# Binary cross-entropy over 8192 x 8192: the first block of predictions loaded by two queues, 64 rows each

## The chip, the cores and the metric

The kernel runs on one core of one Trainium2 chip. The metric is the device time of one execution in microseconds (us). A profile is taken of one further execution, with its own time.

## The reference

```python
def reference(pred, target):
    eps = 1e-7
    pred = np.clip(pred, eps, 1 - eps)
    return -(target * np.log(pred) + (1 - target) * np.log(1 - pred))
```

Both inputs are 8192 x 8192 fp32; `target` holds only zeros and ones. So each element of the result is -log(pred) where the target is 1 and -log(1 - pred) where it is 0. The kernel uses that: it forms |target - 1 + pred|, which is pred or 1 - pred, takes the logarithm and changes the sign.

## The kernel before, in words

The 67,108,864 elements are taken as one flat row and cut into 40 chunks. Chunk `k` is a contiguous stretch of memory, laid out as 128 rows (one for each partition of the on-chip memory) of `widths[k]` elements: two first chunks of 5,120 columns, 35 of 14,336 (`BIG`), two of 5,632 and one of 1,024. Predictions live as fp32 in `ring_p`, which has three slots of 14,336 columns and a small one; the result is made in place there and stored from there. Targets live in `ring_t`, one slot of 14,336 columns and a small one, as bf16: the load converts them, so it reads twice the bytes it writes. The first two chunks lie side by side in one slot of each ring.

The order is written out by hand; nothing is scheduled. For each chunk:

- `load_p` (L69) and `load_t` (L72) bring in predictions and targets. Both are issued by GpSimd (POOL), with one exception: the predictions of chunk 0 are issued by SyncE (SP). All that POOL issues goes through one queue, q0, in the order of issue; SP's transfers use a hardware queue, q1.
- `clip` (L85) on VectorE (DVE).
- `log`: on DVE target - 1 + pred (L91), then on ScalarE (ACT) Abs (L94) and Ln (L95).
- `back` (L99) on DVE multiplies by -1.
- `store` (L76), issued by POOL, for the last chunks by SP. The last chunk goes out by `store_rows` (L81) as three transfers of 108, 12 and 8 rows.

A big chunk is computed in two halves of 7,168 columns. `load_t(k + 1)` stands behind the last L91 of chunk `k`, because there is only one big slot for targets; `load_p(k + 2)` stands behind `store(k)`, since POOL issues in order.

The start, which the change touches, is: a memset of `warm` on DVE; on POOL `load_t(0)`, `load_t(1)`, `load_p(1)`, `load_p(2)`; on SP `load_p(0)`; on ACT a logarithm of `warm` (L108), which loads the table of the function early. Then chunks 0 and 1 are clipped and their logarithms taken, `load_t(2)` is issued, then the sign of chunk 0 is changed and it is stored, and the same for chunk 1.

In what follows p0, p1, p2 are the predictions of chunks 0, 1, 2, and t0, t1, t2 their targets.

Of the kernel before, what the change touches and what calls it, by code (L numbers as in the profile page):

```python
# [1 line left out]

# [4 lines left out]

EPS = 1e-7

BIG = 14 * 1024  # L10
FIRST = 5 * 1024
LAST = 5632
TAIL = 1024
SLOTS = 3


def plan(total):
    n = (total - 2 * FIRST - 2 * LAST - TAIL) // BIG
    assert n > 4 and total == 2 * FIRST + n * BIG + 2 * LAST + TAIL
    spots = [(FIRST, 0, 0), (FIRST, FIRST, FIRST)]  # L20
    spots += [(BIG, k % SLOTS * BIG, 0) for k in range(1, n + 1)]
    end = (n + 1) % SLOTS * BIG
    spots += [(LAST, end, 0), (LAST, end + LAST, LAST)]
    return spots + [(TAIL, SLOTS * BIG, BIG)]


@with_exitstack
def kernel(
    ctx: ExitStack,
    tc: tile.TileContext,  # L30
    pred: bass.AP,
    target: bass.AP,
    out: bass.AP,
):
    nc = tc.nc
    fp32 = mybir.dt.float32
    bf16 = mybir.dt.bfloat16
    Alu = mybir.AluOpType
    Act = mybir.ActivationFunctionType
    P = nc.NUM_PARTITIONS  # L40

    R, C = pred.shape
    spots = plan(R * C // P)
    n = len(spots)
    widths = [s[0] for s in spots]
    cols = [sum(widths[:k]) for k in range(n)]

    def chunk(ap, k):
        flat = ap.rearrange("r c -> (r c)")
        return flat[cols[k] * P : (cols[k] + widths[k]) * P].rearrange("(p w) -> p w", p=P)  # L50

    pool = ctx.enter_context(tc.tile_pool(name="rings", bufs=1))
    ring_p = pool.tile([P, SLOTS * BIG + TAIL], fp32, name="ring_p", tag="ring_p")
    ring_t = pool.tile([P, BIG + TAIL], bf16, name="ring_t", tag="ring_t")
    warm = pool.tile([1, 8], fp32, name="warm", tag="warm")

    def spot(k, part=(0, 1)):
        w, c, _ = spots[k]
        i, m = part
        return ring_p[:, c + i * w // m : c + (i + 1) * w // m]  # L60

    def spot_t(k, part=(0, 1)):
        w, _, c = spots[k]
        i, m = part
        return ring_t[:, c + i * w // m : c + (i + 1) * w // m]

    def load_p(k):
        queue = nc.sync if k == 0 else nc.gpsimd
        queue.dma_start(out=spot(k), in_=chunk(pred, k))  # L69

    def load_t(k):
        nc.gpsimd.dma_start(out=spot_t(k), in_=chunk(target, k))  # L72

    def store(k):
        queue = nc.sync if k >= n - 3 else nc.gpsimd
        queue.dma_start(out=chunk(out, k), in_=spot(k))  # L76

    def store_rows(k):
        src, dst = spot(k), chunk(out, k)
        for first, last in ((0, 108), (108, 120), (120, 128)):  # L80
            nc.sync.dma_start(out=dst[first:last], in_=src[first:last])  # L81

    def clip(k, *part):
        p = spot(k, *part)
        nc.vector.tensor_scalar(  # L85
            out=p, in0=p, scalar1=EPS, scalar2=1 - EPS, op0=Alu.max, op1=Alu.min
        )

    def log(k, *part):
        p = spot(k, *part)  # L90
        nc.vector.scalar_tensor_tensor(  # L91
            out=p, in0=spot_t(k, *part), scalar=1.0, in1=p, op0=Alu.subtract, op1=Alu.add
        )
        nc.scalar.activation(out=p, in_=p, func=Act.Abs)  # L94
        nc.scalar.activation(out=p, in_=p, func=Act.Ln)  # L95

    def back(k, *part):
        p = spot(k, *part)
        nc.vector.tensor_scalar(out=p, in0=p, scalar1=-1.0, scalar2=None, op0=Alu.mult)  # L99

    with tc.manual_schedule():
        nc.vector.memset(warm, 1.0)  # L102
        load_t(0)
        load_p(0)
        load_t(1)
        load_p(1)
        load_p(2)
        nc.scalar.activation(out=warm, in_=warm, func=Act.Ln)  # L108
        for k in (0, 1):
            clip(k)  # L110
            log(k)
        load_t(2)
        back(0)
        store(0)
        back(1)
        store(1)
        load_p(3)
        a, b, c = range(n - 3, n)
        for k in range(2, n - 3):
            for h in (0, 1):  # L120
                clip(k, (h, 2))
                log(k, (h, 2))
            if k < n - 4:
                load_t(k + 1)
            else:
                load_t(a)
                load_t(b)
                load_p(c)
                load_t(c)
                back(k, (0, 2))  # L130
                for j in (a, b):
                    clip(j)
            if k < n - 4:
                back(k, (0, 2))
            back(k, (1, 2))
            store(k)
            if k + 2 < n - 3:
                load_p(k + 2)
            elif k + 2 == n - 3:
                load_p(a)  # L140
                load_p(b)
        log(a, (0, 2))
        log(a, (1, 2))
        clip(c)
        log(b, (0, 2))
        back(a, (0, 2))
        log(b, (1, 2))
        back(a, (1, 2))
        store(a)
        log(c)  # L150
        back(b, (0, 2))
        back(b, (1, 2))
        store(b)
        back(c)
        store_rows(c)


# [1 line left out]
_INS = ['pred', 'target']  # L159
_OUTS = [((8192, 8192), 'float32')]  # L160


# [23 lines left out]
```

## Time and profile before

| | |
|---|---|
| median of 3 runs | 1864.81 us (1864.67 to 1865.51) |
| profiled execution, its own time | 1864.33 us |
| its span, first to last instruction | 1862.6 us |
| DVE busy | 1121.6 us, 60% |
| ACT busy | 902.4 us, 48% |
| POOL busy | 178.5 us, 10% |
| bytes read from HBM, written to it | 536.87 MB, 268.44 MB: 432 GB/s over the span |
| DMA queue q0 (POOL) | 16,704 packets, 662.18 MB, 99.1% of the engines' span |
| DMA queue q1 (SP) | 592 packets, 8.91 MB, 1.1% |

The page names queues by number. A packet of data is one row of a transfer; a few packets of 4 bytes report that a transfer has landed. The column GB/s counts bytes as they are written, so that a load of targets (fp32 read, bf16 written) counts half of what it reads. "DMA" is the mean busy share of the core's 16 DMA engines. "Idle before, releaser" in a line of the timeline is the time for which the engine stood idle before the instruction, and what ended it.

### The profile page before, as it was taken

To read this page: it belongs to the slowest core of one execution; us is meant where nothing else is said; L and a number is where in the kernel's file an instruction comes from. 1 tells how busy PE (TensorE), PEld (TensorE's weight loads), DVE (VectorE), ACT (ScalarE), POOL (GpSimd) and SP (SyncE) were. 2 spreads that over 40 slices of the span, in tenths; PEclk is the share of its full clock that TensorE was granted. 3 is DMA by queue.
4 is the path that set the end of the run, shared out by engine and by line. 5 is a ranking of instruction groups with operands and counts; after the bars stand their busy time and mean duration, and the time that the engine had idled before them with its cause. 6 is when DMAs were issued, how large, how long until landed. Compare 5 with 4: busy or idle time off the path is not lost.

```text
span 1862.6 us, 707 instructions
## 1 busy us (share of the span) xinstructions
DVE 1121.6 (60%) x230; ACT 902.4 (48%) x156; POOL 178.5 (10%) x120
## 2 busy tenths in 40 slices
DVE  4666555555666566555555666566655555666565
ACT  4454444455555544444455555544444445555545
POOL 1111101111110011101111110011101111110020
DMA  9999999999999999999999999999999999999999
GB/s 346 347 371 355 356 352 355 356 355 354 359 375 374 375 372 355 355 355 355 355 355 355 357 374 374 374 372 355 355 356 355 357 357 356 357 373 376 375 352 356
DMA packets 17302, 671.15 MB, mean 360 GB/s; under 512 B 1936, under 2 KB 1936, under 8 KB 2320
## 3 DMA queue, kind: packets, MB, share of 16 engines
q0 software_dynamic: 16704, 662.18, 99.1%
q1 hardware_dynamic: 592, 8.91, 1.1%
q14 instruction: 6, 0.05, 0.0%
HBM read 536.87 MB, written 268.44 MB: 432 GB/s over the span
## 4 chain that ended last, share of the span: by engine, by line
DMA 60%; issue 35%; ACT 3%; DVE 2%; POOL 0%; POOLq 0%; DVEq 0%; PEldq 0%
DMA ring_t<-in_target_dram 57%; DMA ring_p<-in_pred_dram 4%; ACT ring_p L95 1%; ACT ring_p L94 1%; DVE ring_p L91 1%; DVE ring_p L99 0%; DVE ring_p L85 0%; POOL out_dram L76 0%; POOL ring_t L72 0%; POOLq L72 0%; POOL ring_p L69 0%; POOLq L76 0%; DVEq L91 0%; PEldq L181 0%
## 5 line engine op out<-in xcount | busy, mean ns | idle before, releaser
L94 ACT ACTIVATE ring_p<-ring_p 128x7168 f32<-128x7168 f32 (+3 forms) x77 | 452.0, 5870 | 942.1 <-DVE ring_p L91 942.1
L91 DVE SCALAR_TENSOR_TENSOR ring_p<-ring_t,ring_p 128x7168 f32<-128x7168 bf16 (+3 forms) x77 | 558.2, 7251 | 372.5 <-DMA ring_t<-in_target_dram 371.3
L99 DVE TENSOR_SCALAR ring_p<-ring_p 128x7168 f32<-128x7168 f32 (+3 forms) x77 | 285.4, 3706 | 329.4 <-ACT ring_p L95 329.4
L95 ACT ACTIVATE ring_p<-ring_p 128x7168 f32<-128x7168 f32 (+3 forms) x77 | 452.5, 5877 | 2.4
L85 DVE TENSOR_SCALAR ring_p<-ring_p 128x7168 f32<-128x7168 f32 (+3 forms) x75 | 284.6, 3794 | 24.0 <-DMA ring_p<-in_pred_dram 24.0
L76 POOL DMA_DIRECT2D out_dram<-ring_p x37 | 128.0, 3459 | 584.4 <-DVE ring_p L99 584.3
L72 POOL DMA_DIRECT2D ring_t<-in_target_dram x40 | 28.9, 722 | 1057.5 <-DVE ring_p L91 1056.7
L69 POOL DMA_DIRECT2D ring_p<-in_pred_dram x39 | 21.7, 558 | 2.5 <-issue 2.5
L108 ACT ACT_TABLE_LOAD x1 | 1.3, 1283 | 0.7 <-PEq L170 0.7
L102 DVE MEMSET warm<- 1x8 f32 x1 | 0.1, 65 | 0.8 <-PEq L170 0.8
L108 ACT ACTIVATE warm<-warm 1x8 f32<-1x8 f32 x1 | 0.2, 208 | 0.0
L170 POOL MEMSET const-float32-0.0<- 128x1 f32 x1 | 0.1, 99 | 0.2 <-issue 0.2
L170 POOL MEMSET const-bfloat16-1.0<- 128x1 bf16 x1 | 0.1, 102 | 0.0
L170 POOL MEMSET const-float32-1.0<- 128x1 f32 x1 | 0.1, 99 | 0.0
L170 POOL MEMSET const-uint8-127<- 128x1 uint8 x1 | 0.1, 99 | 0.0
## 6 DMA issues: line engine op xcount, KB each, us to landing
ring_p<-in_pred_dram POOLq DMA_DIRECT2D x35, 7168.0 KB, 44.3
out_dram<-ring_p POOLq DMA_DIRECT2D x35, 7168.0 KB, 31.1
ring_t<-in_target_dram POOLq DMA_DIRECT2D x35, 3584.0 KB, 31.3
ring_p<-in_pred_dram POOLq DMA_DIRECT2D x2, 2816.0 KB, 37.2
out_dram<-ring_p SPq DMA_DIRECT2D x2, 2816.0 KB, 14.7
out_dram<-ring_p POOLq DMA_DIRECT2D x2, 2560.0 KB, 28.7
ring_t<-in_target_dram POOLq DMA_DIRECT2D x2, 1408.0 KB, 26.5
ring_p<-in_pred_dram SPq DMA_DIRECT2D x1, 2560.0 KB, 13.1
```

The source lines that it names most:

```text
L69: queue.dma_start(out=spot(k), in_=chunk(pred, k))
L72: nc.gpsimd.dma_start(out=spot_t(k), in_=chunk(target, k))
L76: queue.dma_start(out=chunk(out, k), in_=spot(k))
L85: nc.vector.tensor_scalar(out=p, in0=p, scalar1=EPS, scalar2=1 - EPS, op0=Alu.max, op1=Alu.min)
L91: nc.vector.scalar_tensor_tensor(out=p, in0=spot_t(k, *part), scalar=1.0, in1=p, op0=Alu.subtract, op1=Alu.add)
L94: nc.scalar.activation(out=p, in_=p, func=Act.Abs)
L95: nc.scalar.activation(out=p, in_=p, func=Act.Ln)
L99: nc.vector.tensor_scalar(out=p, in0=p, scalar1=-1.0, scalar2=None, op0=Alu.mult)
L102: nc.vector.memset(warm, 1.0)
L108: nc.scalar.activation(out=warm, in_=warm, func=Act.Ln)
L170: nc = _bacc.Bacc("TRN2", target_bir_lowering=False, num_devices=1)
```

## The change

p0 is loaded by two transfers instead of one. SyncE issues rows (partitions) 0 to 63, ScalarE rows 64 to 127, both at the start; each half is 1,310,720 bytes in rows of 20,480 bytes. On ScalarE the issue stands ahead of the load of the function table and of the logarithm of `warm`. Whoever used the whole of p0, or the slot after it, now waits for two transfers instead of one. Everything else, the order on DVE, POOL and SP included, is as before.

```diff
     def load_p(k):
-        queue = nc.sync if k == 0 else nc.gpsimd
-        queue.dma_start(out=spot(k), in_=chunk(pred, k))
+        if k == 0:
+            for i, queue in enumerate((nc.sync, nc.scalar)):
+                half = slice(i * P // 2, (i + 1) * P // 2)
+                queue.dma_start(out=spot(0)[half], in_=chunk(pred, 0)[half])
+        else:
+            nc.gpsimd.dma_start(out=spot(k), in_=chunk(pred, k))
```

## The prediction

> **What bounds the kernel now.** I read the page first: the strip of 40 slices and the table of queues.
>
> ```profile
> span 1862.6 us, 707 instructions
> DMA  9999999999999999999999999999999999999999
> q0 software_dynamic: 16704, 662.18, 99.1%
> q1 hardware_dynamic: 592, 8.91, 1.1%
> HBM read 536.87 MB, written 268.44 MB: 432 GB/s over the span
> ```
>
> The transfer engines are busy from end to end, while VectorE, the busiest compute engine, is at 60%. To see whether anything could leave them idle I took the medians from issue to landing, and two windows of the middle of the kernel, one period of a big chunk each.
>
> ```profile
> ring_p<-in_pred_dram POOLq DMA_DIRECT2D x35, 7168.0 KB, 44.3
> ring_t<-in_target_dram POOLq DMA_DIRECT2D x35, 3584.0 KB, 31.3
> ...
> 455.18:505.92 50.74, 31.07 (x7) 24.60 (x4) 5.09 (x4) 1.00 1.00 362
> 505.92:556.66 50.74, 30.57 (x7) 24.60 (x4) 4.59 (x4) 1.00 1.00 361
> ```
>
> A period moves 7.34 MB of predictions, 7.34 MB of targets (as read) and 7.34 MB of results: 22.02 MB in 50.74 us, 434 GB/s, or 27.1 GB/s for each of 16 engines; one of the three takes 16.9 us. A load of targets that lands 31.3 us after its issue has therefore waited 14 us behind other transfers, a load of predictions 27 us. So the queue is never empty, and the kernel is one long line of transfers: a step on a compute engine that comes a few us sooner or later changes nothing, and a microsecond that the transfer engines lose at the start is missing at the end. What counts is whether the change costs or gives transfer time. For that I read the first 60 us of the timeline and short windows (the last two columns are the engines' share and GB/s).
>
> ```profile
> 0.74 0.40 SPq L69 DMA_DIRECT2D ring_p<-in_pred_dram  x1
> ...
> 13.88 2.83 DVE L85 TENSOR_SCALAR ring_p<-ring_p 128x5120 f32<-128x5120 f32 x1 [13.02 <-DMA ring_p<-in_pred_dram]
> 16.74 5.49 DVE L91 SCALAR_TENSOR_TENSOR ring_p<-ring_t,ring_p 128x5120 f32<-128x5120 bf16 x1
> ...
> 28.36 2.83 DVE L85 TENSOR_SCALAR ring_p<-ring_p 128x5120 f32<-128x5120 f32 x1 [6.12 <-DMA ring_p<-in_pred_dram]
> ...
> 37.00 2.57 POOL L72 DMA_DIRECT2D ring_t<-in_target_dram  x1 [33.51 <-DVE ring_p L91]
> ```
>
> ```profile
> 2.00:3.00 1.00, 0.00 (x0) 0.23 (x2) 1.00 (x3) 1.00 0.61 184
> 3.00:4.00 1.00, 0.00 (x0) 0.00 (x0) 0.49 (x1) 1.00 1.02 430
> 4.00:5.00 1.00, 0.00 (x0) 0.00 (x0) 0.00 (x0) 1.00 0.91 389
> 5.00:6.00 1.00, 0.00 (x0) 0.00 (x0) 0.00 (x0) 1.00 1.01 307
> 6.00:12.00 6.00, 0.00 (x0) 0.00 (x0) 0.00 (x0) 1.00 1.00 316
> ```
>
> p0 runs alone from about 2 us. At 5 to 6 us GB/s falls: the targets, which count half, have come in from POOL's queue. From 6 to 12 us 316 GB/s at a share of 1.00 is a mixture: with 434 for predictions and 217 for targets, 46% of the engines' time goes to p0, so the two queues take about equal turns. p0 lands at 13.9 us. Then VectorE waits 6.12 us for p1.
>
> **The change part by part.**
>
> *What it gives on paper.* With two queues of three, p0 gets two turns of three instead of one of two. Sharing starts near 5.5 us and ends at 13.9; the same bytes then need three quarters of those 8.4 us, so p0 lands 2.1 us sooner. The clip (2.83 us) starts sooner by as much, but t0 has the place that p0 gave up: the two together have the same bytes as before. By the trace t0 was issued at 1.24 us and landed 14.9 us later, at 16.1, so the first L91 moves from 16.74 to 16.1 at best. ScalarE starts 0.6 us sooner, and all of it ends in the 6.12 us wait for p1, which lands after t0, p0 and t1 whatever their order. Gain on the path: 0.
>
> *ScalarE's issue.* One issue of about 0.40 us (SyncE's row) stands ahead of the table load (1.28 us at 0.73) and the warm logarithm (0.21 us at 2.03). These would end at 2.6 us instead of 2.2; ScalarE's next work waits for L91 until 22.27, so 20 us cover it. Uncovered it would be 0.4 us. The new waits for two transfers where there was one (clip 0, the first Abs, POOL's first store) cost a step of the sequencer, 0.02 us in the chain's rows, all beside running transfers. The time around the span, 1864.33 - 1862.6 = 1.73 us, I leave as it is; no row shows what a second hardware queue adds there.
>
> *The front of the transfers.* From 2 to 3 us the share is 0.61, so 0.39 us is lost, and by the packet records the sixteen first packets take 1.23 us on average instead of 0.76, another 0.5. A second queue could fill some of this: 0 to -0.9 us. It needs the same sixteen engines to start, so I take 0.
>
> *Half-height transfers.* This is the part that decides. How many engines serve a half? q1's 592 packets tell: p0 and the two SyncE stores of 128 rows, and the last chunk's 128 rows, are 512 data packets. Of the 80 left, three transfers of 128 rows with one report from each of 16 engines make 48; the other 32 are the transfers of 108, 12 and 8 rows: 12 + 12 + 8, in each case the largest number up to 16 that divides the rows. 64 rows therefore go to all 16 engines, four rows each. Before, sixteen engines wrote 128 rows at a time, each its own eight; now, whenever their turns coincide, sixteen write into the same 64 rows, and two engines share what one had. If the rows' side takes 27 GB/s for each such group, two engines that are on the same half at once run at half speed. p0 is 2.62 MB, 6.04 us at 434 GB/s. So the cost lies between 0 (the rows' side has room, or the engines always take opposite halves) and +6.04 us (they are always on the same half). The nearest row is the stretch of the last stores, the only ones with fewer rows: 363 GB/s from 1858 to 1860 us at a share of 0.88, or 412 GB/s at full share, 5% under 434. It is near the lower end, but it is a row of reads from the chip's memory, in 4 KB packets, while the engines run out of work, and I don't take it for 20 KB writes. Two queues that start within half a microsecond with the same turn on every engine make coinciding turns the more frequent case, so between half (3.0) and all (6.0) I take three quarters: +4.5 us. Nothing hides it: the line of transfers has no gap to absorb it.
>
> The Trainium skill has a rule that speaks against the change. "SBUF — State Buffer", section "Door 1: The DMA port swizzle", gives 8 of 16 ports for partitions 0 to 63, with 196 GB/s measured at 1 MiB against 328 for 128 partitions, and its section on two DMAs to both halves says that two at once were only 6% faster than one. By that p0 would move at some 208 GB/s, an estimate from that page: 12.6 us instead of 6.04, and the end +6.6 us. No row here shows it.
>
> *What is late next.* p1 would land 4.5 us later, at 32.8; L85 and L91 follow, and t2 is issued at 41.5 instead of 37.00. p2 was issued at 2.95 and took 42.3 us, to 45.2, so t2 had 8.2 us in hand, less the time from issue to first bytes (t0: 1.24 to about 5.5, 4.3 us): 3.9. p2 ends later by the same 4.5, so the margin stays, and no gap is added.
>
> Sum against the profiled execution: 1864.33 + 0 + 0 + 0 + 4.5 = 1868.8 us. Its own time is 0.48 below the median of the runs, so the median could as well come out at 1869.3; I keep 1868.8.
>
> **The rivals.**
>
> *The halves add up* (not slower). If engines on the same half don't hinder each other, every term is 0: 1864.3, or 1864.8 by the median. For it: the equal turns of 6 to 12 us cost no share, and the last stores' row above. Against it: that row is all there is on few rows, and in all full-speed rows each engine has rows of its own. Chance 0.33.
>
> *The front fills faster.* Both sequencers feed the engines, the 0.9 us go: 1863.4. For it the share of 0.61; against it that all 16 engines serve one transfer already. Chance 0.05.
>
> *Both halves on the same eight engines.* If 64 rows went to eight engines, the same for both queues, those would carry 12.08 us of p0 instead of 6.04 and stay 6.04 us behind the others to the end, since every later transfer gives all engines equal shares: 1870.4. It decides as soon as the eight lag by more than the end's 2 us of thin work (share 0.88). Against it is the count of reports. Chance 0.03.
>
> *Something at the front that I don't see makes it faster by over 0.2%.* All that precedes full speed is 2.0 + 0.9 = 2.9 us, under 0.2% (3.7 us). Chance 0.03.
>
> **How the numbers follow.** 0.2%, 3.7 us, is about what a measurement of this kernel can tell from no change. The forecast's case has 0.56: its cost is spread from about 2 to 6.04, and from 62% of p0's packets colliding (3.7 of 6.04) it counts as slower; I give that 0.48 and what lies below 0.08. Slower: 0.48 + 0.03 = 0.51. Same: 0.08 + 0.33 + 0.05 = 0.46. Faster: 0.03. The forecast's own range is 1866.4 to 1870.4. The range for 8 in 10 takes in the rival of no cost, from 1863.9, and the upper bound with the spread of the runs, to 1870.6; both signs of the question lie in it.
>
> **What would show it.** Right: from 2 to 15 us the packets of p0 take longer than 0.76 us and GB/s at full share is well under 389 (2 to 5 us) and 316 (6 to 12 us); p1's clip starts near 32.8 instead of 28.36; from there every row is later by the same amount up to the last store. Wrong: p1's clip at 28.4 and the same period of 50.74 us, with clip 0 at about 11.8. The forecast is also wrong if the front is slow but the lag is gone by the end: then the line of transfers has a gap that I didn't find. A period other than 50.74 would mean that the change reaches beyond the start, for which I see no way.

## The result, and the profile after

| | median, us | runs | against the kernel before, same series |
|---|---|---|---|
| before, with the first series | 1864.81 | 9, 1864.36 to 1865.51 | |
| the change, first series | 1871.27 | 9, 1868.98 to 1878.75 | 1.0041 [1.0033, 1.0049] |
| the change, second series (e5_again) | 1870.17 | 8, 1869.35 to 1871.36 | 1.0027 [1.0017, 1.0037] |
| the change, third series (e8_third) | 1869.83 | 10, 1868.85 to 1870.41 | 1.0025 [1.0016, 1.0035] |

The change makes the kernel slower: by 6.5 us in the first series, by 4.9 in each of the two others (before: 1865.23 and 1864.94). The first series has four runs above 1872 us, the two others none; these four count in its ratio, which is above that of the medians (1.0035). Its profile is that of its slowest run, 1878.75 us with a span of 1877.0.

The page of the changed kernel, strip and queues. (The change moves the lines of the text: the clip is L89 here, target - 1 + pred is L95, `load_t` L76, and p0 is loaded by L71.)

```profile
span 1877.0 us, 713 instructions
DMA  9999999999999999999999999999999999999997
q0 software_dynamic: 16704, 662.18, 98.4%
q1 hardware_dynamic: 528, 7.60, 1.2%
q10 hardware_dynamic: 80, 1.31, 0.3%
HBM read 536.87 MB, written 268.44 MB: 429 GB/s over the span
```

ScalarE's half is q10: 1.31 MB in 80 packets, 64 of data and 16 reports, so 16 engines served 64 rows, as counted in the prediction. The line of transfers is as full as before, and slower. The start of the timeline, and the windows over it (last two columns: the engines' share and GB/s):

```profile
0.73 0.55 ACTq L71 DMA_DIRECT2D ring_p<-in_pred_dram  x1
0.73 0.58 SPq L71 DMA_DIRECT2D ring_p<-in_pred_dram  x1
...
19.05 2.83 DVE L89 TENSOR_SCALAR ring_p<-ring_p 128x5120 f32<-128x5120 f32 x1 [18.19 <-DMA ring_p<-in_pred_dram]
21.91 5.49 DVE L95 SCALAR_TENSOR_TENSOR ring_p<-ring_t,ring_p 128x5120 f32<-128x5120 bf16 x1
...
33.30 2.83 DVE L89 TENSOR_SCALAR ring_p<-ring_p 128x5120 f32<-128x5120 f32 x1 [5.90 <-DMA ring_p<-in_pred_dram]
...
41.95 2.57 POOL L76 DMA_DIRECT2D ring_t<-in_target_dram  x1 [38.47 <-DVE ring_p L95]
```

```profile
2.00:3.00 1.00, 0.00 (x0) 0.81 (x2) 1.00 (x3) 1.00 1.48 328
3.00:4.00 1.00, 0.00 (x0) 0.00 (x0) 0.48 (x1) 1.00 1.44 307
4.00:5.00 1.00, 0.00 (x0) 0.00 (x0) 0.00 (x0) 1.00 0.50 102
5.00:6.00 1.00, 0.00 (x0) 0.00 (x0) 0.00 (x0) 1.00 1.20 246
6.00:12.00 6.00, 0.00 (x0) 0.00 (x0) 0.00 (x0) 1.00 0.93 205
```

Packets count in the window in which they start; over 2 to 6 us the four rows make 0.98 MB, 246 GB/s (328 before), and from 6 to 12 us 205 instead of 316. By the packet records a 20 KB row of p0 takes 1.39 to 1.60 us (medians of sixteen after sixteen) where it took 0.76 to 0.78 after each engine's first one. The mean times of these eight groups of sixteen add up to 11.96 us instead of 6.64: that is what an engine spends on its eight rows. p1's clip, which waits for all that stands ahead of it, comes at 33.30 instead of 28.36: 4.94 us later, and t2 is issued 4.95 later.

So the start costs 4.9 us in a run that is 14.4 us longer than the one before (1864.33). The rest came later. Two targets' loads from the chain that ended last (start in us, length), of the profile before, of this one, and of the third series':

```profile
485.50 31.34 DMA ring_t<-in_target_dram
...
1703.12 31.25 DMA ring_t<-in_target_dram
```

```profile
490.67 31.49 DMA ring_t<-in_target_dram
...
1713.26 32.00 DMA ring_t<-in_target_dram
```

```profile
489.91 31.20 DMA ring_t<-in_target_dram
...
1707.45 31.19 DMA ring_t<-in_target_dram
```

They are 24 chunks apart: a period of 50.73 us before, 50.94 in the first series' profile and 50.73 in the third's. In the first series' profile the load at 490.67 is 5.2 us later than before and the one at 1713.26 is 10.1 us later; the other 4.3 of the 14.4 us come behind it, up to the end.

### The profile page after: what moved, and what is told of

It is laid out like the page before. It is cut to its first block, busy times and chain, and to the rows that moved or that the text cites. A ratio compares the mean times of both kernels' runs of the same rounds, so it can differ in the third digit from the quotient of the medians.

```text
span 1877.0 us, 713 instructions
## 1 busy us (share of the span) xinstructions
DVE 1121.6 (60%) x230; ACT 902.4 (48%) x156; POOL 178.4 (10%) x120
## 3 DMA queue, kind: packets, MB, share of 16 engines
q10 hardware_dynamic: 80, 1.31, 0.3%
## 4 chain that ended last, share of the span: by engine, by line
DMA 60%; issue 35%; ACT 2%; DVE 1%; POOL 0%; POOLq 0%; DVEq 0%; PEldq 0%
DMA ring_t<-in_target_dram 58%; DMA ring_p<-in_pred_dram 2%; ACT ring_p L99 1%; ACT ring_p L98 1%; DVE ring_p L95 1%; DVE ring_p L103 0%; POOL out_dram L80 0%; DVE ring_p L89 0%; POOL ring_t L76 0%; POOLq L76 0%; POOL ring_p L73 0%; POOLq L80 0%; DVEq L95 0%; PEldq L185 0%
## 5 line engine op out<-in xcount | busy, mean ns | idle before, releaser
L95 DVE SCALAR_TENSOR_TENSOR ring_p<-ring_t,ring_p 128x7168 f32<-128x7168 bf16 (+3 forms) x77 | 558.2, 7251 | 378.4 <-DMA ring_t<-in_target_dram 377.1
L89 DVE TENSOR_SCALAR ring_p<-ring_p 128x7168 f32<-128x7168 f32 (+3 forms) x75 | 284.6, 3794 | 29.3 <-DMA ring_p<-in_pred_dram 29.3
L76 POOL DMA_DIRECT2D ring_t<-in_target_dram x40 | 28.9, 722 | 1068.4 <-DVE ring_p L95 1067.6
```

The lines of the kernel that those rows point to most:

```text
L89: nc.vector.tensor_scalar(out=p, in0=p, scalar1=EPS, scalar2=1 - EPS, op0=Alu.max, op1=Alu.min)
L95: nc.vector.scalar_tensor_tensor(out=p, in0=spot_t(k, *part), scalar=1.0, in1=p, op0=Alu.subtract, op1=Alu.add)
```

## The experiments

Ratios are to the kernel before, run beside each.

**e1_columns: two queues, whole height.**

```diff
-                half = slice(i * P // 2, (i + 1) * P // 2)
-                queue.dma_start(out=spot(0)[half], in_=chunk(pred, 0)[half])
+                half = slice(i * FIRST // 2, (i + 1) * FIRST // 2)
+                queue.dma_start(out=spot(0)[:, half], in_=chunk(pred, 0)[:, half])
```

> p0 by two queues as in the change, but cut by columns: SyncE loads columns 0 to 2559 of all 128 rows, ScalarE the other 2560. Same two queues, same bytes. Theory A (sixteen engines writing into 64 rows go at half speed): packets are whole height again, so no cost: p1's clip at 28.4 +- 0.5 us as before (33.30 with the change), median 1864.3 to 1865.5. Rival B (a second hardware queue at the start costs, whatever it carries): p1's clip near 33 us and the median 1869 to 1873 as with the change. Rival C (what is late at the end comes from two queues setting the engines' order, not from the rows): p1's clip near 28.4 but runs spread over several us.

1865.33 us (1864.69 to 1866.52), ratio 1.0001 [0.9992, 1.0010]. Windows and timeline:

```profile
4.00:5.00 1.00, 0.00 (x0) 0.00 (x0) 0.00 (x0) 1.00 1.06 451
5.00:6.00 1.00, 0.00 (x0) 0.00 (x0) 0.00 (x0) 1.00 1.11 338
6.00:12.00 6.00, 0.00 (x0) 0.00 (x0) 0.00 (x0) 1.00 1.02 324
```

```profile
28.54 2.83 DVE L89 TENSOR_SCALAR ring_p<-ring_p 128x5120 f32<-128x5120 f32 x1 [5.96 <-DMA ring_p<-in_pred_dram]
```

The transfers run at full speed, and p1's clip is 0.18 us from where it was. Two hardware queues, two issues, the extra waits and ScalarE's issue ahead of its table load together cost nothing that can be measured. That rules out rival B, and C as far as these runs go.

**e2_one_queue: the same two halves, one queue.**

```diff
-            for i, queue in enumerate((nc.sync, nc.scalar)):
+            for i, queue in enumerate((nc.sync, nc.sync)):
```

> The two transfers of 64 rows both issued by SyncE, one behind the other; ScalarE issues nothing. Theory A (rows): as with the change or more, since no engine can take the other half in between: p1's clip at 33 to 34.5 us, median 1869 to 1873. Rival B (second queue): no cost, p1's clip near 28.4, median 1864.3 to 1865.5.

1870.02 us (1869.69 to 1870.79), ratio 1.0027 [1.0017, 1.0037].

```profile
33.84 2.83 DVE L89 TENSOR_SCALAR ring_p<-ring_p 128x5120 f32<-128x5120 f32 x1 [5.13 <-DMA ring_p<-in_pred_dram]
```

One queue is enough for the whole cost: 5.48 us at p1's clip, 4.85 at the end. With e1 this places it: the cut by rows costs, not the number of transfers or their queues.

**e3_middle_rows: the middle 64 rows by SyncE, the outer 64 by ScalarE.**

```diff
+        if k == 0:
+            for rows, queue in (
+                (slice(32, 96), nc.sync),
+                (slice(0, 32), nc.scalar),
+                (slice(96, 128), nc.scalar),
+            ):
+                queue.dma_start(out=spot(0)[rows], in_=chunk(pred, 0)[rows])
...
```

> SyncE loads rows 32 to 95 of p0 in one transfer, ScalarE rows 0 to 31 and rows 96 to 127 in two. Theory A1 (rows 0 to 63 share half of the paths, rows 64 to 127 the other half): a transfer of 64 rows across the middle reaches all paths and goes at full speed, 0.76 us for a packet of 20 KB, while the two of 32 rows go at half speed; the cost is about half of that of the change: p1's clip near 31 us, median near 1867.5. Theory A2 (fewer than 128 rows at a time are slow, whichever they are): all at half speed or worse, p1's clip at 33 us or later, median 1869 or more. Rival B (the number of transfers or queues): no less than with the change.

1868.60 us (1866.94 to 1870.24), ratio 1.0018 [1.0009, 1.0027]; p1's clip at 31.99, 3.6 us late. The cost is less than that of the change, as A1 has it, but more than half of it, and above what was expected (p1's clip near 31, the median near 1867.5): the outer rows were served first and then mixed with the middle ones (medians of the middle packets 0.96 to 1.44 us). Mixed, the two kinds can't be told apart cleanly, hence e7.

**e7_middle_first: the middle rows alone first, one queue.**

```diff
+        if k == 0:
+            for rows in (slice(32, 96), slice(0, 32), slice(96, 128)):
+                nc.sync.dma_start(out=spot(0)[rows], in_=chunk(pred, 0)[rows])
...
```

> p0 by SyncE alone in three transfers: rows 32 to 95 first, then rows 0 to 31, then 96 to 127. Theory A1 (rows 0 to 63 and 64 to 127 each have half of the paths): the first transfer goes at full speed, 400 GB/s and more from 3 to 5 us and 0.77 us for a packet of 20 KB after each engine's first one; the two others at half speed (1.4 to 1.6 us); p1's clip between 31 and 31.9 us, median 1867.4 to 1868.3. Theory A2 (fewer rows are slow as such): about 210 GB/s from 3 to 5 us, as with 64 rows from row 0, and p1's clip at 33.8 us or later, median 1870 or more.

1867.58 us (1866.29 to 1868.78), ratio 1.0012 [1.0003, 1.0021].

```profile
4.00:5.00 1.00, 0.00 (x0) 0.00 (x0) 0.00 (x0) 1.00 0.91 389
5.00:6.00 1.00, 0.00 (x0) 0.00 (x0) 0.00 (x0) 1.00 1.10 399
6.00:12.00 6.00, 0.00 (x0) 0.00 (x0) 0.00 (x0) 1.00 1.14 232
```

```profile
30.62 2.83 DVE L88 TENSOR_SCALAR ring_p<-ring_p 128x5120 f32<-128x5120 f32 x1 [4.50 <-DMA ring_p<-in_pred_dram]
```

This is the decisive one. A transfer of 64 rows that lies across the middle runs at 389 GB/s from 4 to 5 us, the same as p0 before, and its packets take 0.76 to 0.78 us after each engine's first one; in e2 the transfer of rows 0 to 63 in the same place took 1.37 to 1.61 us for each (medians of sixteen). (The window of 399 GB/s has some rows of targets in it. From 3 to 4 us it is 266, not the expected 400, since the first packets took 1.5 us.) The same engines then take 1.12 to 1.53 us for rows 0 to 31 and 96 to 127. Half the rows are slow, and the cost is about half: 2.26 us at p1's clip, which comes 0.4 us before the expected 31 to 31.9, and 2.35 at the end. A2 falls. (L88 is the clip in this kernel's text.)

**e4_twice: p0 loaded twice, whole height** (2.62 MB more than the kernel needs).

```diff
         queue.dma_start(out=spot(k), in_=chunk(pred, k))
+        if k == 0:
+            spare = ring_p[:, 2 * BIG : 2 * BIG + FIRST]
+            nc.sync.dma_start(out=spare, in_=chunk(pred, 0))
```

> The kernel before, with p0 loaded by SyncE a second time, all 128 rows, into a part of ring_p that is free until later: 2.62 MB more, 6.04 us of the line of transfers at 434 GB/s. It prices what a loss of transfer time at the start is worth at the end. If the line has no gap: p1's clip at 34.4 us, median 1870.6 to 1871.2, runs as close together as before (about 1 us). If a gap takes some of it: under 1870. If a loss at the start by itself makes the end late by more than it is, or makes runs differ: over 1872 or a spread of several us.

1871.53 us (1870.78 to 1871.85), ratio 1.0034 [1.0021, 1.0048].

```profile
34.37 2.83 DVE L88 TENSOR_SCALAR ring_p<-ring_p 128x5120 f32<-128x5120 f32 x1 [10.40 <-DMA ring_p<-in_pred_dram]
```

p1's clip is 6.01 us late (6.04 worked out) and the end 6.4 us, 0.3 above the expected range: no gap in the line takes any of it, and the runs stay close together.

**e5_again, e8_third: the changed kernel twice more.**

> The changed kernel once more, for a second profile: its nine runs lay between 1868.98 and 1878.75 us, and the profiled one, 1878.75, had p1's clip at 33.30 us (4.9 later than before) but the last landing 14 us later. Theory D (two costs: rows at the start, the same in every run, some 5 us; and a drift of the slowest engine behind the others later on, different in each run): p1's clip again near 33.3 us, whatever the end; the end minus 1864.33 minus 4.9 is what the slowest engine's lag grew by beyond the 3 us of before. Rival E (the start itself differs from run to run): a run near 1870 has p1's clip well away from 33.3, by as much as its end differs.

> The changed kernel a third time. So far 17 runs: nine from 1868.98 to 1878.75 (four above 1872), eight from 1869.35 to 1871.36, and two profiles whose start agrees (p1's clip at 33.30 and 33.03 us). Theory D1 (the late drift is chance, in about a quarter of the runs): two or three of these runs above 1872. Theory D2 (the drift belonged to the first series alone, its chip or its moment): none above 1872, median 1869.5 to 1871. In both, p1's clip is between 32.8 and 33.5 us.

The times are in the first table. Second series, then third:

```profile
33.03 2.83 DVE L89 TENSOR_SCALAR ring_p<-ring_p 128x5120 f32<-128x5120 f32 x1 [6.63 <-DMA ring_p<-in_pred_dram]
```

```profile
33.00 2.83 DVE L89 TENSOR_SCALAR ring_p<-ring_p 128x5120 f32<-128x5120 f32 x1 [6.63 <-DMA ring_p<-in_pred_dram]
```

The start is the same in runs of 1869.35, 1870.27 and 1878.75 us, within 0.3 us: theory D, not E. None of the 18 runs is above 1872, as D2 has it: a drift of that size belonged to the first series. Smaller ones stand in e6 and e9 below.

What the drift looks like is in the reports of landing, sixteen for each load, one from each engine. They don't name the engine; I read the same lag in load after load as the same engine's. In the kernel before, in the load of targets issued at 1703.12 us, four of the sixteen engines land 2.1 to 2.8 us behind the median engine; these lags have built up by 600 us and then stay. In the second and third series four and five land 2.0 to 3.4 us behind. In the first series' profile two engines land 7.0 and 9.1 us behind, and the lag was still growing. There, rows of targets that take over 2.3 us instead of 2.13 go on to the end (15 of them between 1000 and 1700 us; none in that stretch in the kernel before, nor in the two later profiles of the change), all among the last three rows of a load to start, when other engines have gone over to the next transfer. What they take over 2.13 us is 5.5 us together, while the two lags grow by 7.3. The lag does not account for all: theory D had the rest of the end's delay equal to what the largest lag grew by, and that is 9.5 against 6.3 us in the first series, 0.1 against 0.6 in the second and 1.0 against -0.2 in the third.

**e6_stagger: engines set apart on purpose** (seven tiny loads that the kernel has no use for).

```diff
+            for i, rows in enumerate((14, 12, 10, 8, 6, 4, 2)):
+                c = 2 * BIG + i * 1280
+                nc.sync.dma_start(
+                    out=ring_p[:rows, c : c + 1280], in_=chunk(pred, 0)[:rows, :1280]
+                )
```

> The change, and behind SyncE's half seven tiny loads of 14, 12, 10, 8, 6, 4 and 2 rows of 5 KB into a part of ring_p that is free until later, so that up to 14 engines are set apart from each other by up to 1.3 us. With the change the engines leave the start close together (last landing reports of p1: 12 of 16 within 0.2 us; before, spread over 0.7). Theory F (being close together is what makes the slowest engine lose time later): runs as close together as before, 1870 to 1872. Rival G (something else of the two queues): runs from 1869 to 1878 as with the change, shifted by up to 1.3 us.

1872.90 us (1872.04 to 1873.52), ratio 1.0040 [1.0028, 1.0053]. This is inconclusive. The runs are close together, but in this series so are those of the plain change, and they lie above the 1870 to 1872 of theory F. At p1's clip the loads cost 0.73 us more than e5 (33.76 us), within the 1.3 allowed for; the median is 2.7 behind e5's. Late in the kernel the most delayed engine is 3.7 us behind the median one (3.4 in e5), and ten rows of targets between 1000 and 1700 us take over 2.3 us.

**e9_swapped: ScalarE rows 0 to 63, SyncE rows 64 to 127.**

> The change with the queues swapped: ScalarE loads rows 0 to 63, SyncE rows 64 to 127. Theory A1 (rows 0 to 63 and 64 to 127 each have half of the paths): nothing changes, p1's clip between 32.8 and 33.5 us, median 1869.5 to 1871.5. Rival (which queue carries which half matters, say because ScalarE's queue is served later): p1's clip off by over 0.5 us, or a median outside of 1869 to 1872.

1871.12 us (1870.30 to 1872.52), ratio 1.0034 [1.0021, 1.0047], p1's clip at 32.78. The start is the same as in e5 and e8 to 0.3 us, and the median lies within what A1 expected. It is 1.3 us above e8's, with the most delayed engine 4.1 us behind the median one late in the kernel instead of 2.6. Since the start is not later, this points to the later lag again, in another series than the first.

## Why the prediction was right or wrong

The time, 1871.27 us, is outside of the range (up to 1870.6). The forecast's sign is right, and so is the term that carries it; the step that failed is the last point of this list.

- *The line of transfers has no gap:* right. e4 puts 6.04 us in and gets 6.0 at p1 and 6.4 at the end.
- *Half-height transfers, +4.5:* right in kind, close in size, and wrong in how I got there. 4.67, 4.64 and 4.94 us in three profiles at p1's clip, 4.9 at the end of two series. But not three quarters of the packets collided with the rest free: in these three profiles none of p0's 128 packets took under 0.9 us. In the four windows from 2 to 6 us the engines served one queue alone, of the first profile and of the second:

```profile
q10 hardware_dynamic: 48, 0.98, 115.5%
```

```profile
q1 hardware_dynamic: 47, 0.96, 108.3%
```

  With all engines on one half there is no opposite half to escape to. That the cost stays under 6.04 has other reasons: before, each engine's first packet took 1.2 us anyway, so only seven of eight had a fast time to lose, and the later packets of the change took 1.22 to 1.47 us (medians), less than twice 0.77. An engine's eight rows took 11.3 to 12.0 us in the three profiles against 6.64 before, 4.7 to 5.3 more.
- *The nearest row:* right to refuse. The last stores' 5% said nothing on loads of 20 KB rows.
- *What it gives on paper:* wrong in the turn. p0 was to land 2 us sooner; its clip came 5.2 us later (19.05 instead of 13.88), so two queues of three never paid. *ScalarE's issue* cost nothing: e1.
- *What is late next:* right. p1's clip at 33.30 (32.8 forecast), t2's issue at 41.95 (41.5), and the windows under 389 and 316 GB/s, all as named for "right".
- *The rivals:* that the halves add up falls with e2; the same eight engines fall with q10's 16 reports; the front did not fill faster, p0's first packet starts at 2.07 us instead of 1.76.
- *The step that failed:* the sum ended at the start. I wrote that I saw no way for a period other than 50.74 us, and gave the spread of the runs 0.2 us (1870.4 to 1870.6). The start alone makes 1864.81 + 4.9 = 1869.7 us, inside the range, and the two later series come to 1870.17 and 1869.83. The first series spreads over 9.8 us, its median is 1.6 us above 1869.7, and its profile has a period of 50.94 us, with two engines that fall further behind from load to load. In that run the later part adds 9.5 us (14.4 - 4.9): 5.2 by 1713 us, 4.3 behind it. That the median's 1.6 us are of the same kind is inferred, since that run has no profile. Nothing of this size is in the 18 later runs. Why those two engines kept losing time is open: e5 and e8 don't show it, e6 can't tell, the lags of 3.7 and 4.1 us in e6 and e9 hint that it is not the first series' alone, and the kernel before ran from 1864.36 to 1865.51 us in the same series.

On the rule of the Trainium skill ("SBUF — State Buffer", "Door 1: The DMA port swizzle"), that partitions 0 to 63 and 64 to 127 have eight ports each: e2 and e7 agree. The 12.6 us that the prediction estimated from that page for p0 are near the 11.3 to 12.0 measured. By the port table that the Trainium skill gives there, rows 32 to 95 reach all sixteen ports, and in e7 they ran at 389 GB/s. The sentence of the Trainium skill on the same page, that only one transfer of all 128 partitions hits all ports ("Can I just issue two DMAs to hit both halves?") does not fit e7. The Trainium skill's "DMA: Bandwidth & Descriptors" says under "Rules for kernel authors" that two halves serialize since they share the engines; e1 shares the engines too and loses nothing, so that can't be the reason here: e2 and e7 say it is the rows.

## What to carry to other kernels

Split a load by columns, or leave it whole. By rows, 32 to 95 ran at full speed and 0 to 63 at about half; but the rows left on either side of the middle were slow too, so that no split by rows was free here (the cheapest, e7, cost 2.4 us). In a kernel whose transfers never pause, price a change at the start in transfer time lost, not in how soon the first work begins: in e2, e3, e4, e7 and the two later series the end came later by what p1's clip had lost, within 0.7 us. That a sooner start would bring nothing is argued, not shown: p0 was computed sooner in none of these runs by more than 0.12 us. And give a range more room where engines run side by side for long: the same change was 4.9 us in two series and 6.5 in a third.

## What the runs showed of the hardware that I had not expected

- Two hardware queues with work at the same time were not taken in turn when their transfers had 64 rows each: 0.98 MB from one and none from the other from 2 to 6 us, in one profile ScalarE's first, in others SyncE's. Transfers of all 128 rows were: in e1, over the same time, 0.65 MB from one and 0.54 from the other. No run shows why.
- By their landing reports the sixteen engines don't run level. In the profile before, four of them are 2 to 3 us behind the median one from 600 us on, by about the same in every load.
